# A two-layer DeltaNet, S5 and MLA backbone with experts: other order of the first loads, of the merged projections, and of the loads behind the first experts

## Chip, cores, metric

The kernel runs on one core of a Trainium2 chip. The metric is the device time of one execution, in microseconds (us), as the median of several runs. A profile of one execution shows what each engine did: TensorE (PE), VectorE (DVE), ScalarE (ACT), GpSimd (POOL), SyncE (SP, which here only issues DMAs), and the 16 DMA engines behind them.

## What is computed

Two layers over 256 latent and 256 context tokens of width 1024, four tiles of 128 tokens in all. Every sub-layer is modulated by shift, scale and gate vectors that come from a small condition vector through a large weight (`ada_w`, 2 x 1024 x 6144).

```python
for i in range(2):
    sh1, sc1, g1, sh2, sc2, g2 = adaln(c, ada_w[i], ada_b[i])     # silu(c) @ ada_w + ada_b, cut in six
    h = rmsnorm(x, norm1_g[i]) * (1 + sc1) + sh1
    if i == 0:      # gated DeltaNet heads beside S5 channel groups, both directions, one output projection
        o = mixer_ab(h_ctx, h_lat, w_in, conv_w, ..., A_re, A_im, log_dt, B, C, D, glu_w, glu_b, w_out)
    else:           # latent attention
        o = mixer_mla(h_ctx, h_lat, w_in, q_norm_g, w_q_up, kv_norm_g, w_kv_up, w_out, cos, sin)
    x = x + g1 * o
    x = x + g2 * grouped_moe(modulate(x), router_w, router_bias, w_gate, w_up, w_down)  # 16 experts, top 2
return rmsnorm(x, final_norm_g)
```

## The kernel before, in words

The program runs through stages, whose bounds in the profiled execution are about these.

- **Start, 0 to 45 us.** `norm0()` normalises and transposes the four token tiles. `ada_gen(0, 0)` loads the first third of layer 0's `ada_w` in 16 chunks of 512 KB (`ch<-in_ada_w`, issued by SP in `load_chunk`) and multiplies each by the condition, which stands in `stat`. `stat` is a copy (L239) of `sg`, which ACT computes from `condT` (L238). `s5_base()` is a long chain of small DVE instructions on the S5 constants `sA` and `sBC`, and ends with `bcr` and `bci`. Behind that chain, in DVE's order, stands `adaev` (L272): the finished modulation plus its bias `adab`, from which PE makes the columns `mcols`. With these DVE and ACT modulate the tokens and the first projection can start on PE.
- **Merged projections, 45 to 345 us.** Five generators (U and S5 tables, S5 matmuls, DeltaNet projections and convolutions, gates, and `loads`, which is the other `ada_gen` parts) are taken one step at a time in the order that the digits of `ORDER` give (`merge`). That order is the order in which each engine gets its instructions. `adab` is filled by two DMAs (L258) ahead of each part, added at the part's end (L272) or, for the part that is cut in two, at its cut (L269).
- **Inverses, 305 to 383 us.** DVE runs a recursion of 31 steps on small triangles (L880 multiplies, L882 reduces; the row lengths grow from step to step up to 961), then two stream transposes (L886, L887), whose result DVE, ACT and POOL copy into `DT` (L1022). `gth` are four gate tiles of the S5 readout (PE, then ACT L972, DVE L973 and L974, POOL stores them, L975). `PI` are starting matrices for the solve (L1040). SP loads the matrices `A` (L1047), `dec` and `qe` in the memory that earlier tiles held, so that its first such load waits for the last DVE read of `gth`.
- **Solve, scan, output projection, routing, 345 to 600 us.**
- **Experts of layer 0, 600 to 875 us.** Weight chunks `ch<-in_wg`, `in_wu`, `in_wd` of 1 MB stream in through SP. A unit writes its result to DRAM by an indirect store (`yd<-y,rt`, L1769). At the end `combine()` loads four tiles `y` of 1 MB back from there, through POOL's queue (L1699), adds their halves on POOL (L1700) and scales and adds them on DVE. The last pair of experts is not stored: its two down weights are multiplied (`down`), and `put_back` spreads the product over the tokens. `open_rg2()` loads the MLA's input weight (`in_mla_w_in`, 4 chunks of 704 KB).
- **MLA, 875 to 1000 us, and experts of layer 1, to 1288.8 us.**

DMAs that are issued by SP and ACT take turns on eight semaphores (in the rows `DMAHW0` to `DMAHW7`), and those of POOL on eight others (`DMASW`): the next DMA on a semaphore is issued only when the one before it has landed. Lines of the changed kernel are one or two higher than those of the kernel before.

Of the kernel before, what the change touches and what calls it, by code (L numbers as in the profile page):

```python
# [10 lines left out]
F32 = mybir.dt.float32  # L11
# [27 lines left out]
ARB = 3  # L39
EA = 0  # L40
HG = (2, 5)
ORDER = "31031442142040140344004440342042144241140004011240243042313341044002441404410432024401434324021044244444244334104124204010344040301240440214420003444442204322414144304030404014104423444410441104234444144032440214301440024230"


def const_arrays():
# [115 lines left out]
def build(tc, I, O):  # L161
    with ExitStack() as es:
        _build(es, tc, I, O)


def _build(es, tc, I, O):
    nc = tc.nc
    V, S, G, T = nc.vector, nc.scalar, nc.gpsimd, nc.tensor

    per = es.enter_context(tc.tile_pool(name="per", bufs=1))  # L170
# [5 lines left out]
    def nm(s):  # L176
        cnt[0] += 1
        return f"{s}_{cnt[0]}"
# [3 lines left out]
    def ps(tag=None):  # L182
        if tag is None:
            tag = banks[0] % banks[1]
            banks[0] += 1
        return psum.tile([128, 512], F32, tag=f"ps{tag}", name=nm("ps"))
# [4 lines left out]
    def chunk(dt=F32):  # L191
        pool = slots[0][slots[1] % len(slots[0])]
        slots[1] += 1
        return pool.tile([128, width[0]], dt, tag="ch", name=nm("ch"))

    def load_chunk(src, shape, eng=nc.sync):
        n = 1
        for s in shape[1:]:
            n *= s
        v = chunk()[:, :n]  # L200
        three = v.rearrange("p (a b) -> p a b", a=shape[1]) if len(shape) == 3 else v
        eng.dma_start(v if len(src.shape) == 2 else three, src)
        return three

    def tp(out, in_, n=128):
        T.transpose(out, in_, ident[:n, :n])

    def mm(out, l, r, start, stop):
        return T.matmul(out, l, r, start=start, stop=stop)  # L209
# [4 lines left out]
    def bcast_rows(src_row, n, parts=128):  # L214
        return bass.AP(tensor=src_row.tensor, offset=src_row.offset, ap=[[0, parts], [1, n]])


    cm = per.tile([128, 7 * 128], F32, name="cm")
    nc.scalar.dma_start(cm, I["c_mats"])
    ident, triF, triB, triS, ones, nmF, nmB = (cm[:, i * 128:(i + 1) * 128] for i in range(7))  # L220
    sm = per.tile([128, 432], F32, name="sm")
    nc.scalar.dma_start(sm, I["c_small"][:, 0:432])
    neghalf = sm[:, SM_NH:SM_NH + 1]
    condT = per.tile([128, 16], F32, name="condT")
    nc.scalar.dma_start(condT, I["condT"])


    def rsqrt(pool, out, ss, n, scale, eps):
        t = pool.tile([128, n], F32, tag=f"rs{n}", name=nm("rs"))
# [10 lines left out]
    adab = per.tile([128, 512], F32, name="adab")  # L240
# [2 lines left out]
    rope = per.tile([128, 2, 2, 32], F32, name="rope")  # L243
    mg = per.tile([128, 5], F32, name="mg")
    n1g = per.tile([128, 2, 8], F32, name="n1g")
    nc.scalar.dma_start(n1g.rearrange("p a b -> p (a b)"), I["norm1_g"])
    mcols = per.tile([128, 2, 2, 2, 8], F32, name="mcols")
    cols1 = per.tile([128, 2, 8], F32, name="cols1")

# [4 lines left out]
    def ada_gen(l, th, ks=range(KD), eng=lambda k: nc.sync):  # L254

        if ks[0] == 0:
            for c in range(2):
                nc.scalar.dma_start(adab[c:128:32, :], I["ada_b"][l, th])  # L258
        p = ps(3)
        for k in ks:  # L260
            for c0 in range(0, 2048, width[0]):
                w = load_chunk(I["ada_w"][l, k * 128:(k + 1) * 128, th * 2048 + c0:th * 2048 + c0 + width[0]],
                               [128, width[0]], eng(k))
                for j in range(width[0] // 512):
                    jj = c0 // 512 + j
                    mm(p[32 * jj:32 * jj + 32, :], stat[:, k, :], w[:, j * 512:(j + 1) * 512], k == ks[0], k == ks[-1])
                yield
        if ks[-1] < KD - 1:
            V.tensor_tensor(adab, p, adab, op=OP.add)  # L269
            return  # L270
        ev = per.tile([128, 512], F32, tag="adaev", name=nm("adaev"))
        V.tensor_tensor(ev, p, adab, op=OP.add)  # L272
        if th == 0:
            p = ps()
            for b in range(4):
                tp(p[:, b * 128:(b + 1) * 128], ev[:, b * 128:(b + 1) * 128])
            pv = p.rearrange("p (b j r) -> p j b r", b=4, j=4)
            for c in range(2):
                V.tensor_copy(mcols[:, l, c, 1].rearrange("p (j b) -> p j b", j=2), pv[:, 0:2, :, c])
                V.scalar_tensor_tensor(mcols[:, l, c, 0].rearrange("p (j b) -> p j b", j=2), pv[:, 2:4, :, c], 1.0,  # L280
                                       n1g[:, l].rearrange("p (j b) -> p j b", j=2), op0=OP.add, op1=OP.mult)
            return
        for c in range(2):
            (nc.scalar if (l, th) == (1, 2) else G).dma_start(modd[l, c, th * 2048:(th + 1) * 2048].rearrange("(j n) -> j n", n=512),
ev[c:128:32, :])
# [42 lines left out]
    def merge(order, *gens):  # L328

        for c in order:  # L330
            next(gens[int(c)], None)
        rr(*gens)
# [5 lines left out]
    def seq(*gens):  # L338
        for g in gens:
            yield from g  # L340
# [50 lines left out]
    qT, kT = (gp.tile([128, 4, 512], F32, tag=n, name=n) for n in ("qT", "kT"))  # L391
    rnq = gp.tile([128, NT, 4], F32, name="rnq")
    convw = gp.tile([128, 12, 5], F32, name="convw")
    nc.scalar.dma_start(convw.rearrange("p a b -> p (a b)"), I["conv_w"])
    gbr = gp.tile([128, 16], F32, name="gbr")
    nc.scalar.dma_start(gbr, bcast_rows(I["gate_b"], 16))
    dng = gp.tile([128, 1], F32, name="dng")
    nc.scalar.dma_start(dng, I["dn_g"].rearrange("a p -> p a"))

    def g32(n):  # L400
        return gp.tile([128, NT, 8], F32, name=n)
# [13 lines left out]
    sp1 = s5st.enter_context(tc.tile_pool(name="sp1", bufs=1, side="right"))  # L415
    sp2 = s5st.enter_context(tc.tile_pool(name="sp2", bufs=2, side="right"))
    sA = sp1.tile([128, 96], F32, name="sA")
    nc.scalar.dma_start(sA, I["s5_A"])
    sBC = sp1.tile([128, 1024], F32, name="sBC")
    nc.scalar.dma_start(sBC, I["s5_BC"])  # L420
    sDl = sp1.tile([128, 8], F32, name="sDl")
    nc.scalar.dma_start(sDl, I["s5_Dl"])
    are, aim = sA[:, 0:32], sA[:, 32:64]
    bcr = sp1.tile([128, 544], F32, name="bcr")
    bci = sp1.tile([128, 544], F32, name="bci")
# [205 lines left out]
    with tc.tile_pool(name="xi1", bufs=1) as xi1, tc.tile_pool(name="ar", bufs=ARB) as arp:  # L631
# [23 lines left out]
        for k in range(KD):  # L655
            for c in range(2):
                a, b = mcols[:, 0, c, 0, k:k + 1], mcols[:, 0, c, 1, k:k + 1]
# [332 lines left out]
    with tc.issue_after(mark.ins):  # L990
        G.memset(X, 0.0)
        rr(with_loads(proj_u()), s5_tables(0))
    yT = pj.tile([128, 4, 512], F32, tag="uy", name="yT")
    merge(ORDER,
          seq(s5_run(0), s5_run(1), s5_run(2), s5_run(3), glu()),
# [20 lines left out]
    for j in range(2):  # L1016
        for d in range(2):
            for b in range(4):
                g0, u0, s_ = 64 * d + 32 * (b // 2), 16 * (b % 2), slice(32 * b, 32 * b + 32)
                src = (Lt if j ^ d else LX)[g0:g0 + 32].rearrange("p k u -> p u k")[:, u0:u0 + 16, :]  # L1020
# [591 lines left out]
    wi, rg2s = [], []  # L1612

    def open_rg2():

        rg2 = es.enter_context(tc.tile_pool(name="rg2", bufs=RG2))
        old, i = slots
        slots[0], slots[1] = [rg2] * RG2, 0
        for j in range(4):
            wi.append(load_chunk(I["mla_w_in"][j], [128, 2, 704]))  # L1620
        slots[0], slots[1] = old, i
        return rg2


    def experts0(m):
        with ExitStack() as st:
# [194 lines left out]
            p = [p for _, _, p in down(cur)]  # L1821
            put_back(p, m.tokf[:, cs], tokm[:, cs], m.gate[:, cs])
            w3s.close()
            rg2s.append(open_rg2())
            last = [rg2s[0].tile([128, 4, 512], F32R, tag="ch", name=f"ch{i}") for i in "hl"]

            def two():
# [208 lines left out]
    with tc.tile_pool(name="l1h", bufs=1) as lh, tc.tile_pool(name="l1i", bufs=2) as li:  # L2036
# [4 lines left out]
        for t in range(NT):  # L2041
            if t + 1 < NT:
                norm_T(1, li, x, hT1, (t + 1,))
            p = ps()
# [22 lines left out]
            p = ps()  # L2067
# [9 lines left out]
            if t >= 2:  # L2077
                p = ps()
# [157 lines left out]
```

## Time and profile before

| | |
|---|---|
| median of 3 runs | 1289.83 us (1289.03 to 1290.67) |
| profiled execution: time | 1290.54 us |
| profiled execution: span of its trace | 1288.8 us |
| PE busy | 1122.1 us (87%) |
| DVE busy | 707.3 us (55%) |
| ACT busy | 437.2 us (34%) |
| POOL busy | 322.1 us (25%) |
| moved by DMA | 340.30 MB, 264 GB/s over the span |
| DMA queue q1 (SP and ACT loads of large rows) / q10 (small rows) / q0 (POOL) | 306.25 / 17.41 / 15.50 MB |

The time of an execution is 1.7 us more than the span, from the first to the last instruction that the trace holds. PE is the busiest engine, but its share is an average over stages: it is near its limit in the merged projections and the experts, and waits at the start, in the inverses and at the end of the first experts.

### The profile page before, as it was taken

How to read it: one execution, taken by the hardware profiler on the slowest of the kernel's cores; microseconds unless marked ns; L12 is line 12 of the kernel's file. 1: busy time of each engine (PE TensorE's matmuls, PEld its weight loads, DVE VectorE, ACT ScalarE, POOL GpSimd, SP SyncE). 2: the span in 40 equal slices, each digit the busy share in tenths (PEclk: the TensorE clock that was granted, in tenths of full speed). 3: DMA queues.
4: the chain of work that ended last, by engine and by line, in shares of the span. 5: the costliest groups of instructions: out<-in, count | busy, mean ns of one | idle time of the engine just before them, and what ended most of it. 6: DMA issues, size and time to landing. Idle time of an engine off the chain costs nothing. (4 is left out here: it accounts for less than half of the span.)

```text
span 1288.8 us, 17198 instructions
## 1 busy us (share of the span) xinstructions
PE 1122.1 (87%) x6208; PEld 706.1 (55%) x6208; DVE 707.3 (55%) x1452; ACT 437.2 (34%) x763; POOL 322.1 (25%) x263
## 2 busy tenths in 40 slices
PE   4698999999759998769999999867999949999985
PEld 1365566565229987626567577325777735444321
DVE  3979796847694564742347478245576260223122
ACT  3323535352123242213446467205455111111101
POOL 0355453321236330312133233133321010000000
PEclk9799999999878998879999999978999959999998
DMA  9565576887738154658999999753134758999992
GB/s 329 196 196 179 198 225 204 251 289 227 223 129 279 59 187 148 253 201 361 399 380 418 396 419 388 268 221 121 59 124 148 292 220 356 417 419 421 420 421 123
DMA packets 101784, 340.30 MB, mean 264 GB/s; under 512 B 26806, under 2 KB 44598, under 8 KB 75328
## 3 DMA queue, kind: packets, MB, share of 16 engines
q1 hardware_dynamic: 75792, 306.25, 62.9%
q10 hardware_dynamic: 20128, 17.41, 4.3%
q0 software_dynamic: 5776, 15.50, 3.1%
q8 instruction: 51, 0.84, 0.3%
q14 instruction: 37, 0.30, 0.1%
HBM read 318.40 MB, written 25.72 MB: 267 GB/s over the span
## 5 line engine op out<-in xcount | busy, mean ns | idle before, releaser
L1684 DVE TENSOR_TENSOR lo<-ch,hi 128x1024 fp32r<-128x1024 f32 x80 | 112.1, 1443 | 57.2 <-ACT hi L1682 57.1
L209 PE MATMUL ps<-hi,sp 128*128 128x512 f32 x432 | 112.4, 399 | 1.3 <-ACT y L1767 1.3
L209 PE MATMUL ps<-ch,stat 128*32 128x512 f32 x384 | 89.3, 652 | 24.3 <-DVE stat L239 14.0
L209 PE MATMUL ps<-ch,xT 128*64 128x512 f32 (+1 forms) x488 | 108.7, 596 | 1.3 <-DMA ch<-in_wg 1.3
L209 PE MATMUL ps<-ch,wh 128*64 128x512 f32 x384 | 100.9, 631 | 6.7 <-SPq L1592 6.7
L1682 ACT ACTIVATE hi<-ch 128x1024 fp32r<-128x1024 f32 x96 | 94.3, 1056 | 35.5 <-DMA ch<-in_wg 27.3
L209 PEld LDWEIGHTS ps<-hi,sp 128*128 128x128 f32 x432 | 79.4, 188 | 27.1 <-issue 5.7
L209 PE MATMUL ps<-hH,wh 128*128 128x512 f32 x160 | 66.2, 415 | 5.9 <-ACT hH L664 5.1
L209 PE MATMUL ps<-hH,wl 128*128 128x512 f32 x160 | 65.2, 408 | 1.6 <-DVE wl L611 1.6
L209 PE MATMUL ps<-hL,wh 128*128 128x512 f32 x160 | 65.7, 410 | 0.4 <-POOL hL L665 0.2
L209 PE MATMUL ps<-lo,sp 128*128 128x512 f32 x216 | 63.7, 403 | 2.5 <-DVE lo L1684 1.5
L209 PEld LDWEIGHTS ps<-ch,xT 128*64 128x64 f32 (+1 forms) x488 | 33.3, 129 | 59.3 <-issue 55.2
L209 PEld LDWEIGHTS ps<-ch,wh 128*64 128x64 f32 x384 | 28.9, 144 | 65.7 <-issue 62.1
L1684 POOL TENSOR_TENSOR lo<-ch,hi 128x1024 fp32r<-128x1024 f32 x16 | 42.4, 2647 | 87.2 <-ACT hi L1682 62.9
L231 POOL TENSOR_TENSOR frs<-rs,sm 128x1 f32<-128x1 f32 x2 | 1.1, 548 | 241.2 <-DVE rs L230 241.2
L209 PE MATMUL ps<-ch,aT 128*64 128x512 f32 (+1 forms) x232 | 55.9, 613 | 3.9 <-DMA ch<-in_wd 3.2
L209 PEld LDWEIGHTS ps<-lo,sp 128*128 128x128 f32 x216 | 39.1, 188 | 16.7 <-issue 3.2
L611 POOL TENSOR_TENSOR wl<-raw,wh 128x1024 fp32r<-128x1024 f32 x16 | 39.7, 2479 | 27.7 <-ACT wh L610 27.6
L1919 DVE SCALAR_TENSOR_TENSOR y<-ps,rt,bcm 128x512 f32<-128x512 f32 x14 | 10.5, 752 | 65.2 <-PE ps L209 65.2
L1151 POOL TENSOR_TENSOR ch<-ch,ch 128x512 fp32r<-128x512 f32 (+1 forms) x28 | 31.8, 1165 | 53.7 <-PE ps L209 29.9
L748 DVE SCALAR_TENSOR_TENSOR ac<-ps,convw,ac 128x510 f32<-128x510 f32 (+1 forms) x48 | 35.6, 741 | 13.3 <-ACT ac L744 12.9
L209 PEld LDWEIGHTS ps<-ch,stat 128*32 128x32 f32 x384 | 12.9, 113 | 54.3 <-DMA ch<-in_ada_w 24.8
(542 smaller groups left out, 2368.6 us busy)
## 6 DMA issues: line engine op xcount, KB each, us to landing
ch<-in_wg SPq DMA_DIRECT2D x63, 1024.0 KB, 13.7
ch<-in_wu SPq DMA_DIRECT2D x62, 1024.0 KB, 10.2
ch<-in_wd SPq DMA_DIRECT2D x61, 1024.0 KB, 12.2
ch<-in_ada_w SPq DMA_DIRECT2D x88, 512.0 KB, 4.8
raw<-in_w_in SPq DMA_DIRECT2D x16, 512.0 KB, 3.5
bcm<-modd ACTq DMA_DIRECT2D x12, 512.0 KB
x<-in_xs SPq DMA_DIRECT2D x8, 512.0 KB, 8.2
yd<-x SPq DMA_DIRECT2D x8, 512.0 KB, 4.9
```

What stands on the lines that cost most here:

```text
L209: return T.matmul(out, l, r, start=start, stop=stop)
L231: G.tensor_tensor(out, t, bc(neghalf, [128, n]), op=OP.pow)
L611: eng.tensor_tensor(wl, w, wh.bitcast(F32), op=OP.subtract)
L748: V.scalar_tensor_tensor(ac[:, :, lo:hi], pv[:, :, lo + o:hi + o], convw[:, blk, j:j + 1], ac[:, :, lo:hi], op0=OP.mult, op1=OP.add)
L1151: eng.tensor_tensor(lo, src, hi.bitcast(F32), op=OP.subtract)
L1682: S.activation(hi[:, s], w[:, s], AF.Copy)
L1684: e.tensor_tensor(lo[:, s], w[:, s], hi[:, s].bitcast(F32), op=OP.subtract)
L1919: V.scalar_tensor_tensor(y, p, j.gate, g2[:, nh * 512:(nh + 1) * 512], op0=OP.mult, op1=OP.mult)
```

## The change

There are three parts.

1. The condition `condT` is issued as the first DMA of ACT's queue, ahead of `cm` and `sm`. Seven small constants (`n1g`, `convw`, `gbr`, `dng`, `sA`, `sBC`, `sDl`) and the twelve `adab` loads are issued by POOL in place of ACT.
2. `ORDER` is another string with the same number of each digit (50, 30, 30, 24 and 90 of 0 to 4).
3. The four `in_mla_w_in` loads are issued after the last load of `in_wd`, through `issue_after`.

```diff
-ORDER = "31031442142040140344004440342042144241140004011240243042313341...
+ORDER = "41040414313243010242003024140101404241444403141443434244404024...
...
+    issued = [None]
+
     def load_chunk(src, shape, eng=nc.sync):
...
-        eng.dma_start(v if len(src.shape) == 2 else three, src)
+        issued[0] = eng.dma_start(v if len(src.shape) == 2 else three, src)
...
+    condT = per.tile([128, 16], F32, name="condT")
+    nc.scalar.dma_start(condT, I["condT"])
     cm = per.tile([128, 7 * 128], F32, name="cm")
     nc.scalar.dma_start(cm, I["c_mats"])
...
-    condT = per.tile([128, 16], F32, name="condT")
-    nc.scalar.dma_start(condT, I["condT"])
-
...
-    nc.scalar.dma_start(n1g.rearrange("p a b -> p (a b)"), I["norm1_g"])
+    G.dma_start(n1g.rearrange("p a b -> p (a b)"), I["norm1_g"])
...
             for c in range(2):
-                nc.scalar.dma_start(adab[c:128:32, :], I["ada_b"][l, th])
+                G.dma_start(adab[c:128:32, :], I["ada_b"][l, th])
...
-    nc.scalar.dma_start(sA, I["s5_A"])
+    G.dma_start(sA, I["s5_A"])
...
-    nc.scalar.dma_start(sBC, I["s5_BC"])
+    G.dma_start(sBC, I["s5_BC"])
...
-            rg2s.append(open_rg2())
+            with tc.issue_after(issued[0].ins):
+                rg2s.append(open_rg2())
```

**ACT at the program's start.** The rows are ACT's instructions in their order, before; what stands in brackets is what an instruction waits for.

```order
L219 DMA cm<-in_c_mats 128x896
L222 DMA sm<-in_c_small 128x432
L225 DMA condT<-in_condT 128x16
L246 DMA n1g<-in_norm_g 128x16
L394 DMA convw<-in_conv_w 128x60 [waits DMAHW1_49]
L396 DMA gbr<-in_gate_b 128x16 [waits DMAHW3_49]
L398 DMA dng<-in_dn_g 128x1 [waits DMAHW5_49]
L418 DMA sA<-in_s_A 128x96 [waits DMAHW7_49]
L420 DMA sBC<-in_s_BC 128x1024 [waits DMAHW1_49]
L238 ACT_TABLE_LOAD
L238 ACTIVATE sg<-condT 128x16
```

The same place of the changed kernel:

```order
L221 DMA condT<-in_condT 128x16
L223 DMA cm<-in_c_mats 128x896
L226 DMA sm<-in_c_small 128x432
L239 ACT_TABLE_LOAD
L239 ACTIVATE sg<-condT 128x16 [waits DMAHW0_49]
L291 ACTIVATE junk_157,ss_155<-x_144 128x1024 [waits DMAHW1_49]
L1982 DMA rope<-in_c_rope 128x128
```

Five DMAs that wait for earlier DMAs stood ahead of `sg`; now none does. The seven constants stand at the head of POOL's order, without a wait, and a pair of `adab` loads stands behind them.

**DVE around the `adab` addition.** The rows are DVE's, before, in the late steps of the recursion (`x_144` holds the triangles).

```order
L880 TENSOR_TENSOR x_144<-x_144 128x484
L882 TENSOR_REDUCE x_144<-x_144 128x22
L269 TENSOR_TENSOR adab<-ps_2953,adab 128x512
L880 TENSOR_TENSOR x_144<-x_144 128x529
L882 TENSOR_REDUCE x_144<-x_144 128x23
```

In the changed kernel:

```order
L881 TENSOR_TENSOR x_144<-x_144 128x676
L270 TENSOR_TENSOR adab<-ps_2904,adab 128x512
L883 TENSOR_REDUCE x_144<-x_144 128x26
L881 TENSOR_TENSOR x_144<-x_144 128x729
L883 TENSOR_REDUCE x_144<-x_144 128x27
```

The addition stood after step 22; now three whole steps and half of a fourth (23 to 26) stand ahead of it.

**DVE at the end of the recursion.** Before, from the last multiplication on:

```order
L880 TENSOR_TENSOR x_144<-x_144 128x961
L974 TENSOR_TENSOR gth_3287<-yT,gth_3287 128x512
L882 TENSOR_REDUCE x_144<-x_144 128x31
L1040 COPY PI_3359<-cm 128x512
L1040 COPY PI_3363<-cm 128x512
L973 TENSOR_SCALAR gth_3297<-gth_3297 128x512
L886 STREAM_TRANSPOSE x_144<-x_144 128x1024
L887 STREAM_TRANSPOSE x_144<-x_144 128x1024
L974 TENSOR_TENSOR gth_3297<-yT,gth_3297 128x512
L1022 COPY DT<-x_144 32x16x32 x4
```

In the changed kernel:

```order
L883 TENSOR_REDUCE x_144<-x_144 128x31
L887 STREAM_TRANSPOSE x_144<-x_144 128x1024
L888 STREAM_TRANSPOSE x_144<-x_144 128x1024
L974 TENSOR_SCALAR gth_3287<-gth_3287 128x512
L1023 COPY DT<-x_144 32x16x32 x4
L1041 COPY PI_3359<-cm 128x512
L975 TENSOR_TENSOR gth_3287<-yT,gth_3287 128x512
L1041 COPY PI_3363<-cm 128x512
L974 TENSOR_SCALAR gth_3297<-gth_3297 128x512
L975 TENSOR_TENSOR gth_3297<-yT,gth_3297 128x512
```

The two `PI` copies and half a `gth` pair no longer stand ahead of the transposes; the last two `gth` pairs now stand behind the `DT` copies. On ACT the `gth_3297` activation (L973) has moved behind ACT's eight `DT` copies in the same way.

**SP at the end of the first experts.** Before (the `ISA` rows put an expert's number in an address):

```order
L202 DMA ch_6699<-in_wu 128x2048
L202 DMA ch_6803<-in_mla_w_in 128x1408
L202 DMA ch_6805<-in_mla_w_in 128x1408
L202 DMA ch_6807<-in_mla_w_in 128x1408
L202 DMA ch_6809<-in_mla_w_in 128x1408
L202 ISA
L202 DMA ch_6740<-in_wd 128x2048
```

In the changed kernel:

```order
L204 DMA ch_6740<-in_wd 128x2048
L204 ISA
L204 DMA ch_6742<-in_wd 128x2048
L204 ISA
L204 DMA ch_6753<-in_wd 128x2048
L204 ISA
L204 DMA ch_6755<-in_wd 128x2048
L204 DMA ch_6803<-in_mla_w_in 128x1408
```

The four down weights are now issued ahead of the four mixer weights. The first mixer load waited for PE and DVE (its memory is that of the experts' last split weights); the first down weight waits for one of these DVE instructions, not for PE.

## Rows read from the trace of the kernel before

**Rows 1.** Windows: bounds, length, busy PE PEld DVE ACT POOL (x), PEclk, DMA share, GB/s

```profile
100.00:200.00 100.00, 93.29 (x748) 62.10 (x748) 84.13 (x161) 43.90 (x95) 52.17 (x41) 1.00 0.60 194
...
345.00:400.00 55.00, 34.38 (x159) 20.96 (x158) 41.47 (x45) 17.42 (x27) 26.69 (x21) 0.78 0.59 204
...
830.00:875.00 45.00, 25.45 (x62) 7.68 (x58) 19.28 (x21) 0.66 (x2) 12.97 (x8) 0.78 0.56 229
```

**Rows 2.** Timeline of ACT and its queue at the start: start, length, engine, line

```profile
1.65 0.45 ACTq L225 DMA_DIRECT2D condT<-in_condT  x1
...
13.50 0.21 ACT L238 ACTIVATE sg<-condT 128x16 f32<-128x16 f32 x1
```

**Rows 3.** Timeline of PE at the start (in brackets: idle before, releaser)

```profile
13.98 1.94 PE L209 MATMUL ps<-ch,stat 128*32 128x512 f32 x8 [13.98 <-DVE stat L239]
...
39.59 1.05 PE L209 MATMUL ps<-ch,stat 128*32 128x512 f32 x4 [0.21 <-DMA ch<-in_ada_w]
```

**Rows 4.** Timeline of DVE at the start, first and last of the chain

```profile
22.03 0.17 DVE L347 TENSOR_SCALAR exdt<-sA 128x32 f32<-128x32 f32 x1
...
43.28 0.68 DVE L272 TENSOR_TENSOR adaev<-ps,adab 128x512 f32<-128x512 f32 x1
```

**Rows 5.** Windows as in rows 1: the start, and a stretch of weight loading

```profile
4.00:40.00 36.00, 19.46 (x94) 6.14 (x96) 19.35 (x106) 12.85 (x21) 2.21 (x4) 1.00 0.96 354
...
830.00:840.00 10.00, 4.15 (x16) 1.27 (x12) 0.69 (x1) 0.60 (x1) 2.91 (x4) 0.91 1.01 416
```

**Rows 6.** Timeline of POOL, its first weight split

```profile
45.69 2.39 POOL L611 TENSOR_TENSOR wl<-ch,wh 128x1024 fp32r<-128x1024 f32 x1 [3.49 <-ACT wh L610]
```

**Rows 7.** Timeline of DVE in the recursion's late steps

```profile
353.09 0.69 DVE L269 TENSOR_TENSOR adab<-ps,adab 128x512 f32<-128x512 f32 x1 [7.87 <-DMA ch<-in_glu_w]
...
360.98 0.86 DVE L882 TENSOR_REDUCE x<-x 128x26 f32<-128x676 f32 x1
...
373.74 0.42 DVE L973 TENSOR_SCALAR gth<-gth 128x512 f32<-128x512 f32 x1
...
375.81 0.68 DVE L974 TENSOR_TENSOR gth<-yT,gth 128x512 f32<-128x512 f32 x1
...
377.48 2.55 DVE L1040 COPY PI<-cm 128x512 f32<-128x512 f32 x2
...
380.28 1.89 DVE L886 STREAM_TRANSPOSE x<-x 128x1024 f32<-128x1024 f32 x1
```

**Rows 8.** Timelines of ACT, SP and DVE behind the transposes

```profile
374.08 0.69 ACT L972 ACTIVATE gth<-ps,glub 128x512 f32<-128x512 f32 x1 [3.02 <-DMA c5d<-gth]
...
382.26 8.54 ACT L1022 COPY DT<-x 32x512 f32<-32x512 f32 x8 [6.44 <-DVE x L886]
...
383.97 0.38 SPq L1047 DMA_DIRECT2D A<-atd  x1
...
391.49 0.69 DVE L1082 TENSOR_TENSOR dec<-ps,dec 128x512 f32<-128x512 f32 x1 [2.19 <-DMA dec<-dcd]
```

**Rows 9.** Timelines of SP and POOL at the end of the first experts

```profile
825.38 2.04 SPq L202 DMA_DIRECT2D ch<-in_mla_w_in  x4
827.62 4.26 SPq L202 DMA_DIRECT2D ch<-in_wd  x4
...
826.35 0.97 POOL L1769 DMA_INDIRECT yd<-y,rt  x1 [6.28 <-ACT y L1767]
835.48 2.91 POOL L1699 DMA_DIRECT2D ch<-yd  x4 [8.16 <-issue]
847.72 2.34 POOL L1700 TENSOR_TENSOR ch<-ch 128x1024 f32<-128x1024 f32 x1 [9.32 <-DMA ch<-yd]
```

**Rows 10.** POOL's twelve indirect stores: from issue to landing

```profile
DMA to landing us min/median/max: 4.2/9.2/13.3
```

**Rows 11.** What PE waited for (60 to 345 us), and who waited for `adab` loads

```profile
PE ps L209 <- DMA ch<-in_ada_w: 6.0, 7, 2.9
...
  ACT vt L750: 9.8, 1
```

More of the change, by code (lines that the diff above doesn't have):

```diff
@@ L41 @@
 HG = (2, 5)
-ORDER = "31031442142040140344004440342042144241140004011240243042313341044002441404410432024401434324021044244444244334104124204010344040301240440214420003444442204322414144304030404014104423444410441104234444144032440214301440024230"
+ORDER = "41040414313243010242003024140101404241444403141444434244404024011202020010013333444144244340402442214333040144420001444414402120400440240432041400242344403004041344444414231420440044444414114343442210204014240240143442403320"
 def const_arrays():
@@ L393, in _build @@
     convw = gp.tile([128, 12, 5], F32, name="convw")
-    nc.scalar.dma_start(convw.rearrange("p a b -> p (a b)"), I["conv_w"])
+    G.dma_start(convw.rearrange("p a b -> p (a b)"), I["conv_w"])
     gbr = gp.tile([128, 16], F32, name="gbr")
-    nc.scalar.dma_start(gbr, bcast_rows(I["gate_b"], 16))
+    G.dma_start(gbr, bcast_rows(I["gate_b"], 16))
     dng = gp.tile([128, 1], F32, name="dng")
-    nc.scalar.dma_start(dng, I["dn_g"].rearrange("a p -> p a"))
+    G.dma_start(dng, I["dn_g"].rearrange("a p -> p a"))
     def g32(n):
@@ L417, in _build @@
     sA = sp1.tile([128, 96], F32, name="sA")
-    nc.scalar.dma_start(sA, I["s5_A"])
+    G.dma_start(sA, I["s5_A"])
     sBC = sp1.tile([128, 1024], F32, name="sBC")
-    nc.scalar.dma_start(sBC, I["s5_BC"])
+    G.dma_start(sBC, I["s5_BC"])
     sDl = sp1.tile([128, 8], F32, name="sDl")
-    nc.scalar.dma_start(sDl, I["s5_Dl"])
+    G.dma_start(sDl, I["s5_Dl"])
     are, aim = sA[:, 0:32], sA[:, 32:64]
```

## Prediction

> **What bounds the kernel now.** I read the busy time by windows first, then the timelines at the three places that the change touches, then the table of waits between them. In the windows [rows 1] the reader is to see that the stages differ: in the merged projections PE is busy 93.29 of 100 us, so what comes earlier there stays earlier; from 345 to 400 us it is busy 34.38 of 55 and from 830 to 875 us 25.45 of 45, so there something else ends last. The first 45 us are a race between loads and a DVE chain. ACT reaches `sg` only at 13.50 although `condT` was issued at 1.65 [rows 2], and PE begins at 13.98 [rows 3]. That idle time is not the loss, though. PE then catches up with the loads: its last chunk at 39.59 waits for a DMA again [rows 3]. The end of the stage is `adaev` at 43.28 [rows 4], 2.64 us after that chunk's matmuls end (39.59 + 1.05), because DVE first has to finish the S5 constants, a dense chain that starts at 22.03 and is 21.25 us long up to `adaev`.
>
> **Part 1, the start.** Moving instructions off ACT's queue lets `sg` go as soon as `condT` lands. What this is worth is set by the later of two ends.
> DVE's chain: `sA` is the fifth POOL DMA, and POOL takes 2.91 / 4 = 0.73 us to issue one [rows 9], so it leaves at about 0.7 + 5 x 0.73 = 4.4. No row shows how soon such a load lands; the nearest are POOL's indirect stores, 4.2 to 13.3 us [rows 10]. So the chain starts between 8.6 and 17.7 and gets to `adaev` between 29.9 and 39.0, in either case ahead of 40.64. The 2.64 us go.
> Loads: from 4 to 40 us 36 us at 354 GB/s = 12.7 MB were moved, with the DMA engines busy 0.96 of the time [rows 5]. If only the idle 4% can be won, the last chunk comes 1.4 us earlier; if the rate rises to the 416 GB/s of the later stretch [rows 5], 12.7 MB take 30.6 us, 5.4 less. SP will have fewer waits on shared semaphores, but the same small rows travel; I take 3.0. Sum of part 1: 2.64 + 3.0 = about 5.5 us, with 0 (the loads no faster and the chain late) and 8 as ends.
> What it adds: a pair of `adab` loads on POOL, waiting for DVE to read the old `adab`, now stands ahead of POOL's first weight split. The split itself waited for ACT until 45.69 [rows 6], 2.41 us after `adaev` began; `adaev`'s 0.68 and two issues of 0.73 make 2.14, so ACT's wait covers it. If ACT too came earlier by 1 us, the cost would be 0.7. I take nothing for it.
> At this point the Trainium skill speaks against the change. "DMA: Bandwidth & Descriptors" (Rules for kernel authors) says that spreading DMAs over several issuing engines buys no bandwidth, since all share the same 16 DMA engines, and saves only issue time. By that rule the load term would be near the 1.4 us of idle share and part 1 would be worth 4.0; the 0.96 is a row that leans to it, and it is the second rival's ground below.
>
> **Part 2, the new ORDER.** PE's work is the same and nearly in the same places, so I cost the inverses' end, where DVE is behind. Before, DVE stood 7.87 us at the `adab` addition, until 353.09, for the last `ada_w` matmuls [rows 7]. Now the steps that ran from 353.78 (353.09 + 0.69) to 360.98 [rows 7], 7.2 us, stand ahead of it, so the wait shrinks to 0.7. From 377.48 to 380.28 two `PI` copies and a `gth` half stood ahead of the transposes, 2.8 us, and the pair of `gth_3287` (0.42 + 0.68 at most, 0.9 with their overlap) moves behind too [rows 7]. The transposes so start 7.2 + 2.8 + 0.9 = 10.9 us earlier, at 369.4 on the old time scale.
> Most of this goes back. SP's first `A` load left at 383.97 [rows 8], when DVE had read the last `gth`. ACT copies `DT` for 8.54 us, from 2.0 us after the first transpose starts (382.26 against 380.28) [rows 7, 8]; `gth_3297` now stands behind these copies. So: 369.4 + 2.0 + 8.5 = 379.9 for ACT's copies, 0.7 for the `gth` activation [rows 8], 1.1 for its two DVE instructions, and `A` leaves at 381.7 instead of 383.97. What the solve waits for behind it, down to `dec` at 391.49, which waits for a load issued after `A` [rows 8], follows by the same 2.3 us. Lower end: the new sequence can cost PE waits elsewhere. PE lost 6.0 us to `ada_w` chunks between 60 and 345 us [rows 11], and a redrawn order moves these either way; I give it half of them, 3. Upper end: 10.9 if ACT's `gth` does not hold `A`, which the order excludes; 5.3 with a gain in the projections. I take 2.5, from -1 to 5.5.
>
> **Part 3, the mixer's loads.** Before, SP stood at the first `in_mla_w_in` until 825.38, and the four down weights left from 827.62 on [rows 9]. The store issued at 826.35 met this burst: POOL came to its four `y` loads 8.16 us after issuing it, at 835.48 [rows 9], while the shortest of the twelve stores landed in 4.2 [rows 10]. The first sum of `y` began at 847.72 [rows 9], and PE's spreading and DVE's additions to 875 stand behind it. Now the first down weight leaves once DVE's split is done, before PE's end at 825.4, the others follow as PE frees their buffers, and the mixer's 2.8 MB (4 x 704 KB) come last. So the store has the DMA engines nearly alone for its first 2 us; I estimate 4.7 us instead of 8.2, so `y` leaves and the chain behind it runs 3.5 us earlier. Ends: 8.16 - 4.2 = 4.0; and 0, or a loss of 1, if the down weights now share with the store as the mixer's did. The mixer's weights come later, but have some 45 us until the norm ends; this cover holds.
>
> **Sum.** 5.5 + 2.5 + 3.5 = 11.5 us off the profiled 1290.54 gives 1279.0; its own median was 0.7 lower, so I forecast 1278.5 us.
>
> **Rivals.**
> - *Only part of it* (0.22). The start stays bound by its loads (4.0 or less), and either the merge's gain or the store's comes to nothing. For it: the share of 0.96 and the 8.5 us that part 2 hands back. Against it: three independent terms. 1289.8 - 3 to 8 us: 1282 to 1287, in the middle 1284.5.
> - *More* (0.10): loads at 416 GB/s (8), merge 5.5, store 4.0, so 17.5 off: 1272; with a clock on PE that doesn't fall around 345 us (PEclk is 0.78 there [rows 1]) down to 1268.
> - *No change* (0.08): the freed time reappears as waiting in the projections, within 0.2%, 2.6 us, about what a measurement of this kernel can tell.
> - *Slower* (0.12): POOL's queue. An `adab` load waits for DVE to read the old bias; before, it held ACT for 9.8 us once [rows 11], and ACT had nothing urgent. On POOL it holds weight splits, which take 2.39 us [rows 6] and feed PE. Five more pairs are issued; two stand directly ahead of a split. If each holds its split by 9.8 us less the 2.4 that ACT's wait covers, PE loses 14.8 us against 11.5 won: 1293. It decides once such waits sum to over 11.5 us. Against it: the waits are at the end of an `ada_gen` part, and most other splits are spread well apart from these.
> The Trainium skill has a second mechanism for this rival: "SBUF — State Buffer" (SBUF: two separate sides) says that while DVE runs certain copies GpSimd cannot write descriptors, so that DMAs from its queue stand still. No run here shows it yet; it would lengthen the same holds.
>
> **How the numbers follow.** The forecast's case, a gain of 8 to 16 us, 1274 to 1282, has 0.48. With 0.10 above and 0.22 below, faster by over 0.2% has 0.80, the same 0.08, slower 0.12. A range of 1269 to 1287 leaves out the slower case, most of the unchanged one and little of the largest gains, about 2 in 10.
>
> **What would show it.** Start: `sg` before 8 us, the DVE chain done before the last chunk, `adaev` at 37 to 39 us and released by PE. Inverses: the wait at the `adab` addition under 2 us, transposes directly behind the last step, and `A` released by `gth_3297`, some 12 us behind the transposes. End of experts: down weights from 822 on, the store landed within 5 us, the first sum at about 844 less the earlier gains. Wrong would be: `adaev` still released by DVE's own order, PE waiting for `wl` behind an `adab` issue on POOL, or the store still at 8 us beside the down weights.

## The result, and the profile after the change

| | before | after |
|---|---|---|
| median (lowest to highest, 7 runs each) | 1289.83 us (1281.38 to 1295.66) | 1281.9 us (1277.56 to 1286.09) |
| profiled execution, time / span | 1290.54 / 1288.8 us | 1283.03 / 1281.2 us |

The ratio is 0.9947, with a 95% interval from 0.9923 to 0.9971: 6.8 us of 1289.83, faster by more than 0.2%. The forecast was 1278.5 us.

The two traces, read at the same instructions, give this account (the last column is what each stretch adds to the gain):

| instruction | before | after | gained so far | in this stretch |
|---|---|---|---|---|
| `adaev`, DVE | 43.28 | 43.09 | 0.2 | |
| first projection, PE | 50.28 | 49.69 | 0.6 | 0.6 |
| first stream transpose, DVE | 380.28 | 366.91 | 13.4 | 12.8 |
| first load of `A`, SP | 383.97 | 380.51 | 3.5 | -9.9 |
| routing starts, DVE | 539.35 | 535.45 | 3.9 | 0.4 |
| last store of the first experts, POOL | 826.35 | 819.98 | 6.4 | 2.5 |
| `y` loads, POOL | 835.48 | 823.74 | 11.7 | 5.3 |
| first matmul of the MLA's norm, PE | 877.89 | 867.22 | 10.7 | -1.0 |
| routing of layer 1, PE | 1029.56 | 1020.23 | 9.3 | -1.4 |
| end of the span | 1288.8 | 1281.2 | 7.6 | -1.7 |

**The start.** ACT's timeline, against [rows 2], then PE's [rows 3] and DVE's [rows 4]:

```profile
5.25 0.21 ACT L239 ACTIVATE sg<-condT 128x16 f32<-128x16 f32 x1 [1.82 <-DMA condT<-in_condT]
15.31 1.06 ACT L291 ACTIVATE junk<-x 128x1024 bf16<-128x1024 f32 x1 [1.80 <-DMA x<-in_xs]
16.36 4.25 ACT L641 ACTIVATE x<-x,rs 128x1024 f32<-128x1024 f32 x4
...
16.73 1.92 PE L211 MATMUL ps<-ch,stat 128*32 128x512 f32 x4 [16.73 <-DVE rs L231]
40.21 1.05 PE L211 MATMUL ps<-ch,stat 128*32 128x512 f32 x4 [0.23 <-DMA ch<-in_ada_w]
...
16.56 0.15 DVE L231 TENSOR_SCALAR rs<-ss 128x1 f32<-128x1 f32 x1 [1.48 <-ACT junk L291]
16.63 0.17 DVE L348 TENSOR_SCALAR exdt<-sA 128x32 f32<-128x32 f32 x1
20.66 0.69 DVE L646 COPY x<-ps 128x512 f32<-128x512 f32 x1 [2.75 <-ACT x L641]
22.88 0.69 DVE L646 COPY x<-ps 128x512 f32<-128x512 f32 x1 [1.21 <-PE ps L208]
23.76 0.69 DVE L646 COPY x<-ps 128x512 f32<-128x512 f32 x1
26.90 0.69 DVE L646 COPY x<-ps 128x512 f32<-128x512 f32 x1 [1.34 <-PE ps L208]
43.09 0.68 DVE L273 TENSOR_TENSOR adaev<-ps,adab 128x512 f32<-128x512 f32 x1
```

`sg` goes 8.25 us earlier, and DVE's chain starts 5.4 us earlier, yet `adaev` is where it was. Copies of transposed tokens (L646) stand in DVE's order between the chain's instructions. Before the change the first of them was done ahead of the chain, and the other three stood inside it without a wait of their own:

```profile
21.15 0.69 DVE L645 COPY x<-ps 128x512 f32<-128x512 f32 x1
24.45 0.68 DVE L645 COPY x<-ps 128x512 f32<-128x512 f32 x1
26.46 0.69 DVE L645 COPY x<-ps 128x512 f32<-128x512 f32 x1
28.47 0.69 DVE L645 COPY x<-ps 128x512 f32<-128x512 f32 x1
```

Now the chain has come to them before the tokens are ready. It waits 2.75 + 1.21 + 1.34 = 5.3 us for normalisations (L641) that all stand behind ACT's sum of squares of the fourth token tile (15.31). From its first instruction to `adaev` it takes 26.46 us instead of 21.25, and the difference is about these waits. The chain's own start, too, is set by that tile: the `rs` ahead of it (16.56) waits for the same sum, while `sA`, issued at 3.63, had landed 8.5 us later. PE's first `ada_w` matmul is not held by DVE, whose `stat` copy was done at 5.7; the `rs` that its row names only ended last. Its chunk, issued at 5.24, took 11.4 us to land. The matmul begins 2.75 us later than before, and the last chunk comes at 40.21 instead of 39.59. The window against [rows 5]:

```profile
4.00:40.00 36.00, 20.01 (x92) 6.48 (x92) 19.79 (x106) 11.77 (x20) 4.78 (x12) 0.95 0.95 347
```

The loads moved at 347 GB/s against 354, with the DMA engines busy 0.95 against 0.96 of the time.

**The inverses.** DVE's and ACT's timelines, SP's first load, and PE's first matmul with `A`, against [rows 7, 8]:

```profile
350.35 0.69 DVE L270 TENSOR_TENSOR adab<-ps,adab 128x512 f32<-128x512 f32 x1 [2.20 <-PE ps L211]
366.91 1.90 DVE L887 STREAM_TRANSPOSE x<-x 128x1024 f32<-128x1024 f32 x1
...
368.88 5.32 ACT L1023 COPY DT<-x 32x512 f32<-32x512 f32 x5 [3.31 <-DMA Kn<-knd]
374.22 3.25 ACT L1023 COPY DT<-x 32x512 f32<-32x512 f32 x3
377.49 0.69 ACT L973 ACTIVATE gth<-ps,glub 128x512 f32<-128x512 f32 x1
...
379.75 0.69 DVE L975 TENSOR_TENSOR gth<-yT,gth 128x512 f32<-128x512 f32 x1
380.51 0.38 SPq L1048 DMA_DIRECT2D A<-atd  x1
383.51 2.05 PE L211 MATMUL ps<-DT,A 128*128 128x128 f32 x8 [16.72 <-DMA A<-atd]
```

The reader sees the handing back in four rows: the transposes at 366.91, ACT's `DT` copies to 377.47, the `gth` that waited behind them, and `A` 13.6 us behind the transposes, where before it was 3.7.

**The end of the first experts.** SP and POOL, against [rows 9]:

```profile
815.81 9.70 SPq L204 DMA_DIRECT2D ch<-in_wd  x4
...
819.98 0.97 POOL L1770 DMA_INDIRECT yd<-y,rt  x1 [6.28 <-ACT y L1768]
823.74 2.91 POOL L1700 DMA_DIRECT2D ch<-yd  x4 [2.78 <-issue]
836.03 2.33 POOL L1701 TENSOR_TENSOR ch<-ch 128x1024 f32<-128x1024 f32 x1 [9.38 <-DMA ch<-yd]
841.83 2.35 POOL L1701 TENSOR_TENSOR ch<-ch 128x1024 f32<-128x1024 f32 x1 [3.47 <-DMA ch<-yd]
```

POOL's wait for the store fell from 8.16 to 2.78 us. The first sum still waits 9.38 us for its loads, and the next ones now wait too.

### The profile page after: what moved, and what is told of

Read it like the earlier page. It is cut to its first block, busy times and chain, and to the rows that moved or that the text cites. A ratio compares the mean times of both kernels' runs of the same rounds, so it can differ in the third digit from the quotient of the medians.

```text
span 1281.2 us, 17228 instructions
## 1 busy us (share of the span) xinstructions
PE 1116.6 (87%) x6208; PEld 705.5 (55%) x6208; DVE 705.8 (55%) x1452; ACT 439.2 (34%) x764; POOL 332.7 (26%) x282
## 5 line engine op out<-in xcount | busy, mean ns | idle before, releaser
L211 PE MATMUL ps<-ch,wh 128*64 128x512 f32 x384 | 95.6, 604 | 0.7 <-ACT wh L1664 0.7
L211 PEld LDWEIGHTS ps<-ch,stat 128*32 128x32 f32 x384 | 13.6, 116 | 64.2 <-issue 32.5
L1152 POOL TENSOR_TENSOR ch<-ch,ch 128x512 fp32r<-128x512 f32 (+1 forms) x28 | 31.5, 1155 | 53.8 <-PE ps L211 29.9
```

The lines of the kernel that those rows point to most:

```text
L1152: eng.tensor_tensor(lo, src, hi.bitcast(F32), op=OP.subtract)
```

## The experiments

Each was timed beside the kernel before on the same chip; the change itself is in the last row. The kernel before had medians of 1289.82 us beside the first four rows, 1289.70 beside the next four and 1288.42 beside the four after them, so medians from different groups compare less well than ratios. The ratio is not the quotient of two medians, and the two can differ by 2 or 3 us. "Noted" columns are from the profiled execution: first projection on PE, first transpose on DVE, first `DT,A` matmul on PE, routing on DVE, and the `y` loads on POOL.

| kernel | median us (runs) | ratio to before, 95% | projection | transpose | `DT,A` | routing | `y` loads |
|---|---|---|---|---|---|---|---|
| only part 1 | 1296.34 (12) | 1.0044 [1.0022, 1.0065] | 49.47 | 377.55 | 395.40 | 548.01 | 848.05 |
| only part 2 | 1296.8 (12) | 1.0045 [1.0022, 1.0069] | 52.26 | 384.65 | 397.57 | 551.71 | 845.59 |
| only part 3 | 1287.33 (12) | 0.9958 [0.9932, 0.9983] | 50.64 | 384.85 | 391.24 | 543.73 | 831.08 |
| parts 2 and 3 | 1292.12 (12) | 1.0020 [0.9991, 1.0049] | 52.42 | 381.14 | 393.94 | 547.65 | 835.98 |
| all, `dec` x3 | 1279.74 (9) | 0.9928 [0.9902, 0.9954] | 49.01 | 371.30 | 375.52 | 534.63 | 822.97 |
| before, `dec` x3 | 1286.27 (12) | 0.9986 [0.9962, 1.0010] | 50.52 | 380.37 | 387.08 | 539.43 | 833.72 |
| part 1, `dec` x3 | 1288.49 (12) | 0.9997 [0.9973, 1.0020] | 49.49 | 380.10 | 385.30 | 543.91 | 837.83 |
| all, mixer behind `y` | 1281.75 (12) | 0.9946 [0.9924, 0.9969] | 50.15 | 365.26 | 382.23 | 535.77 | 827.57 |
| all, copies on ACT | 1284.67 (12) | 0.9969 [0.9950, 0.9989] | 47.45 | 366.40 | 383.30 | 536.26 | 830.99 |
| all, `dec` x3, copies on ACT | 1278.03 (6) | 0.9913 [0.9884, 0.9941] | 48.30 | 372.41 | 376.62 | 535.02 | 823.34 |
| parts 2 and 3, `dec` x3 | 1286.5 (12) | 0.9976 [0.9950, 1.0002] | 50.20 | 377.72 | 382.97 | 543.38 | 838.42 |
| all, `adab` on ACT | 1286.54 (12) | 0.9990 [0.9965, 1.0015] | 47.20 | 376.93 | 389.80 | 540.47 | 828.85 |
| all (the change) | 1281.9 (7) | 0.9947 [0.9923, 0.9971] | 49.69 | 366.91 | 383.51 | 535.45 | 823.74 |

**The parts apart.** Four kernels with one or two of the three parts of the change:

```diff
 only part 1: the kernel before, and
+    condT ahead of cm and sm; G.dma_start for seven constants and adab
 only part 2: the kernel before, and
+ORDER = "41040414313243010242003024140101404241444403141443434244404024...
 only part 3: the kernel before, and
+            with tc.issue_after(issued[0].ins):
+                rg2s.append(open_rg2())
 parts 2 and 3: the changed kernel, with part 1 taken back
```

Part 1 alone: 

> The kernel before with part 1 alone (condition first, small constants on POOL's queue). Theory A, from the two traces: the DVE chain starts earlier but then stands behind the four token copies, adaev comes at about 43 as before, so ratio 0.999 to 1.001, under 1.5 us. Theory B, as predicted: 5.5 us, ratio 0.996, with adaev at 37 to 39.

Part 2 alone: 

> The kernel before with the new ORDER alone. Theory A: 2 to 3.5 us faster, ratio 0.9975; the transposes start 10 us or more earlier, the first A load only 2 to 3.5 us earlier. Theory B (the trace's gain up to 345 us was chance or came from part 1): ratio 1.000.

Part 3 alone: 

> The kernel before with the mixer's loads behind the down weights alone. Theory A: POOL's wait for the last store shrinks from 8.2 to about 3 us and the time falls by 4 to 5.5 us, ratio 0.996. Theory B (the y loads and not the store set the end, what is won is given back behind the mixer's later weights): under 1.5 us.

Parts 2 and 3: 

> The changed kernel without part 1 (old start, new ORDER, mixer's loads behind the down weights). Theory A: as fast as the full change within 1.5 us, ratio to the kernel before 0.994 to 0.996. Theory B, part 1 pays in the full change: slower than it by 3 us or more, ratio 0.997 or above.

Only part 3 pays by itself: 5.4 us by the ratio (1289.82 x 0.0042), with 2.2 to 8.8 us by its interval, while the medians differ by 2.5. Its place shows the same mechanism as in the changed kernel, a wait of 2.77 us between the last store and the `y` loads. Part 1 alone and part 2 alone make the kernel 5.7 and 5.8 us slower, and parts 2 and 3 together are not told from before. Added up, the three parts give 6 us in the wrong direction; together they give 6.8 us. The idea that the parts add fell; parts 1 and 2 without part 3 were not run. The theories missed the time of part 1 alone and of part 2 alone, since none had a loss; in the place the first theory of part 1 held, with `adaev` at 42.87. For part 3 the first theory held, for parts 2 and 3 the second. The profiled execution of part 1 alone was the slowest of its twelve (1303.92), so its trace shows the places better than the sizes. Part 1 alone loses behind the transposes, where ACT and SP of that kernel show

```profile
389.97 0.69 ACT L973 ACTIVATE gth<-ps,glub 128x512 f32<-128x512 f32 x1
392.19 0.38 SPq L1048 DMA_DIRECT2D A<-atd  x1
395.40 2.04 PE L211 MATMUL ps<-DT,A 128*128 128x128 f32 x8 [8.78 <-DMA A<-atd]
```

The last `gth` stands behind ACT's `DT` copies there without any new `ORDER`, and `A` goes 14.6 us after the transposes. Part 2 alone keeps the two `PI` copies ahead of its transposes (at 384.65), so `ORDER` alone does not bring the sequence that the prediction costed.

**The wait of `A` for `gth`.** The first `A` lies in memory that the readout's tiles held. `dec`, which shares its pool, had four buffers; with three, `A`'s address moves out of there:

```diff
-        dec = eA.tile([128, 4, 128], F32, tag="dec", name=nm("dec"))
+        dec = eA.tile([128, 4, 128], F32, tag="dec", bufs=3, name=nm("dec"))
```

In the changed kernel: 

> The changed kernel with three buffers for dec in place of four, so that the memory of the first A load no longer reaches into that of yT, which the last gth addition reads. Theory A (A's wait for the last gth addition sets the end of the inverses): the first A load leaves before 345 us instead of 380.5, the first solve matmul starts at 377 to 379 instead of 383.5, when the DT copies are done, and the time falls by 4 to 6 us, ratio to the kernel before 0.990. Theory B (the solve is bound by the DT copies and the PI matrices anyway): under 1.5 us below the change, ratio 0.994.

In the kernel before: 

> The kernel before with three buffers for dec. There A left 3.7 us behind the transposes and ACT's DT copies ended at 390.8, after A's landing at 386.9. Theory A: the copies take over the wait, 0 to 2 us faster, ratio 0.999. Theory B (the loads, wherever they stand, cost the same): 4 us or more faster, ratio 0.997 or less.

With part 1 alone: 

> The kernel before with part 1 alone and three buffers for dec. Theory A (part 1 alone loses because the old ORDER then puts the last gth addition 14.6 us behind the transposes): 5 to 7 us faster than part 1 alone, ratio to the kernel before 0.999 in place of 1.0044. Theory B (it loses in the projections): ratio 1.003 or more.

The load leaves at 339.87, 348.12 and 354.07 in the three kernels. In the changed kernel PE's and DVE's timelines become

```profile
375.52 2.05 PE L211 MATMUL ps<-DT,A 128*128 128x128 f32 x8 [5.07 <-ACT DT L1023]
379.80 2.05 PE L211 MATMUL ps<-DT,A 128*128 128x128 f32 x8 [2.23 <-DVE DT L1023]
386.29 2.04 PE L211 MATMUL ps<-PI,DT 128*128 128x128 f32 x8 [4.44 <-DVE PI L1072]
...
383.76 1.73 DVE L975 TENSOR_TENSOR gth<-yT,gth 128x512 f32<-128x512 f32 x1
385.41 0.73 DVE L1072 COPY_PREDICATED PI<-lvl,ps 128x512 f32<-128x512 int32 x1
```

The first `DT,A` matmul is 8.0 us earlier than in the changed kernel, although the transposes come 4.4 us later here (371.30 against 366.91). The matmul with `PI` is only 2.3 us earlier (388.54 there): the wait moves to the `DT` copies and then to DVE, where the same `gth` now stands ahead of `PI`. Routing is 0.8 us earlier, the medians differ by 2.2 us, between the two theories, and the intervals overlap. Before the change the copies end as late as `A`, so the edit gives nothing at this place (387.08 against 386.90). With part 1 alone it wins 10.1 us there (395.40 to 385.30) and 4.1 us at routing, and the ratio goes from 1.0044 to 0.9997. So most of what part 1 loses alone goes when `A` is freed, and the wait of `A` is the likely place; the edit moves other instructions too, such as the transposes from 377.55 to 380.10.

**Parts 2 and 3 with `A` freed.** The same line of `dec` in the kernel with parts 2 and 3:

> Parts 2 and 3 without part 1, and dec in three buffers. Theory A (ORDER without part 1 loses only at A's wait for the last gth): as dec3, with the start of the kernel before, so 1280.5, ratio 0.993. Theory B (it loses ahead of the inverses, since the same string gives the engines another order when the DMAs of part 1 are on other queues): the transposes stay near 381 instead of 367, routing comes near 545 instead of 535, and the time is about 1289, ratio 0.999.

The second theory held in the place: the transposes come at 377.72, 10.8 us behind the change, and routing at 543.38, 7.9 us behind. In the time the ratio of 0.9976 rules out the first theory's 0.993. But `A` counts here as well: against parts 2 and 3 without the edit, the first `DT,A` matmul comes 11.0 us earlier (393.94 to 382.97), routing 4.3 us earlier, and the ratio falls from 1.0020 to 0.9976, though the intervals overlap. Without part 1 the new `ORDER` loses ahead of the inverses, and, as far as these two runs show, at `A` too. The profiled execution was the slowest of its twelve (1295.64, median 1286.50).

**Which piece of part 1 the `ORDER` needs.** In the changed kernel, only the `adab` loads go back to ACT:

```diff
-                G.dma_start(adab[c:128:32, :], I["ada_b"][l, th])
+                nc.scalar.dma_start(adab[c:128:32, :], I["ada_b"][l, th])
```

> The changed kernel with only the twelve adab loads back on ACT's queue; condT stays first and the seven constants stay on POOL. Theory A (what ORDER needs of part 1 is the adab loads, which recur through the merged projections, on POOL): the transposes come at 375 to 381 as without part 1, and the time is 1290 to 1292, ratio 1.000 to 1.002. Theory B (it needs the start alone): transposes at 367, adab's addition with a wait of 2 us, ratio 0.995.

The first theory held in the place and about in the size, if with a time somewhat below what it gave: transposes at 376.93 in place of 366.91, and no gain that can be told from zero, although this kernel has the earliest first projection of all (47.20). Its DVE has the two `PI` copies ahead of the transposes again, and PE waits twice as long for `ada_w` chunks between 45 and 345 us. DVE's timeline and PE's waits of this kernel, and behind the dots PE's waits of the changed one (total, times, longest):

```profile
374.33 2.69 DVE L1041 COPY PI<-cm 128x512 f32<-128x512 f32 x2
376.93 1.89 DVE L887 STREAM_TRANSPOSE x<-x 128x1024 f32<-128x1024 f32 x1
...
PE ps L211 <- DMA ch<-in_ada_w: 12.4, 12, 2.0
...
PE ps L211 <- DMA ch<-in_ada_w: 6.1, 8, 2.8
```

SP shows a likely cause: here it stands up to 12.6 us at one staging store (L863, in the rows a wait for the tile `x`), in the changed kernel 2.4 at most. The three other kernels with the new `ORDER` and without the `adab` loads on POOL show the same pair: up to 10.8 to 12.5 us at that store, and 10.0 to 10.7 us of PE's waits for `ada_w` chunks. No run changes the store alone. The program is built with `schedule_with_timeline_sim=True` (L2232 of the kernel before): a scheduler draws each engine's order from its own model of the times, so an `ORDER` string can mean another order on the engines as soon as a DMA changes its queue, as DVE's order does here.

**The chain at the start.** In the changed kernel the four copies of tokens that DVE makes go to ACT; the orders of PE, POOL and SP stay the same:

```diff
-                    (V.tensor_copy if h else S.copy)(hT[:, 4 * h:4 * h + 4, t], h4(p))
+                    S.copy(hT[:, 4 * h:4 * h + 4, t], h4(p))
```

> The changed kernel with the four DVE copies of transposed tokens at the start (L646) put on ACT beside ACT's own four; the orders of PE, POOL and SP are the same as in the changed kernel. Theory A (part 1 gained so little because these copies, and the waits ahead of them, stand inside DVE's S5 chain): the chain loses 2.8 us of copies and 5.3 us of waits, adaev is released by PE right behind the last ada_w chunk at about 41.4 us instead of 43.09, the first projection starts near 48.0 instead of 49.69, and the time falls by 1.7 us to about 1280.2 (ratio 0.993). Theory B (the chain is held elsewhere, or the start is covered behind): adaev stays at 43, or comes earlier without any change of the time (0.9947).

With `dec` in three buffers too:

> The kernel before this one with dec in three buffers as well, so that the load of A needs no memory of gth. If the two gains are independent (theory A): 1281.9 - 2.2 - 1.7 = 1278.0, ratio 0.991, below both kernels. If what is won at the start is lost in the merged projections or at the transposes (theory B): 1279.7 as with dec alone, ratio 0.993.

DVE and PE of the first of these:

```profile
37.57 0.68 DVE L490 TENSOR_TENSOR bci<-bci,tmpb 128x512 f32<-128x512 f32 x1
40.90 0.69 DVE L273 TENSOR_TENSOR adaev<-ps,adab 128x512 f32<-128x512 f32 x1 [2.65 <-PE ps L211]
47.45 1.22 PE L211 MATMUL ps<-hH,wh 128*128 128x512 f32 x2 [5.15 <-ACT hH L665]
```

The chain ends at 38.25, and PE releases `adaev`, as the first theory had it; the first projection is 2.24 us earlier, of which some 0.4 us are the loads', whose last chunk came at 39.80 in this execution. The time did not follow: 0.9969 is no better than 0.9947, and the intervals overlap. Of the 2.24 us 0.8 are left at the third `adaev`, 0.5 at the transposes and 0.2 at the first `DT,A` matmul, so the merged projections take the start's gain back. With `dec` in three buffers the median is the lowest of all, 1278.03 us of only 6 runs, ratio 0.9913; whether the copies add to `dec` (1279.74) is open, since both lie within the other's interval. Both versions have lower medians than the change, and clearly lower than the kernel before.

**The mixer's loads behind the `y` loads.** POOL issues both, one behind the other:

```diff
-            with tc.issue_after(issued[0].ins):
-                rg2s.append(open_rg2())
+            with tc.issue_after(ylast.ins):
+                rg2s.append(open_rg2(G))
```

> The changed kernel with the mixer's four loads issued by POOL behind its four y loads, in place of SP behind the down weights. Theory A (the y loads, which share the DMA engines with the mixer's 2.8 MB, set the end of the first experts): the last y sum starts 5 to 7 us earlier, the norm of the MLA too, ratio to the kernel before 0.990. Theory B (only the store's landing counts): no change against 0.9947, or a loss if the mixer's weights come too late for the MLA.

```profile
827.57 2.94 POOL L1700 DMA_DIRECT2D ch<-yd  x4 [2.78 <-issue]
830.51 2.13 POOL L204 DMA_DIRECT2D ch<-in_mla_w_in  x4
838.71 2.33 POOL L1701 TENSOR_TENSOR ch<-ch 128x1024 f32<-128x1024 f32 x1 [6.08 <-DMA ch<-yd]
841.27 8.84 POOL L1701 TENSOR_TENSOR ch<-ch 128x1024 f32<-128x1024 f32 x3 [0.23 <-DMA ch<-yd]
```

Here the sum's wait falls from 9.38 to 6.08 us and the other sums follow without a gap, 3 us won at this place; the time is the change's, 0.9946 to 0.9947. In this execution the store came 3.8 us later for another reason (last section). Up to the first matmul of the MLA's norm the 3 us are kept: it begins at 867.92, 0.7 us behind the change. Why the medians show nothing of them stays open.

## Why the prediction was right, and where it was not

The time was right: 1281.9 us against 1278.5, between 1269 and 1287, and faster. The sum of 11.5 us that made it came out as 6.8 to 7.9, and one of its three terms failed. That the time still lies well inside the range is partly luck: in the two traces part 3 gave 1.8 us more than predicted, and 2.2 us came from the landing of a load that the change does not touch (last section).

**Part 1 (5.5 us predicted, 0.6 in the trace).** Two steps failed. "So the chain starts between 8.6 and 17.7 and gets to `adaev` between 29.9 and 39.0": it started at 16.63, inside these bounds, but not for their reason: `sA` had landed at about 12.1, and the fourth token tile held the chain. And its length did not stay 21.25 us. Of the four token copies three stood inside it before as well, but there the tokens were ready; started earlier, it waits 5.3 us for them. The experiment with the copies on ACT shows that these copies and their waits were all that kept `adaev` behind PE. The prediction's own sign of being wrong, `adaev` still released by DVE's own order, is what the trace shows. "I take 3.0" for the loads: the last chunk came 0.6 us later instead of 3.0 earlier. On this the rule of "DMA: Bandwidth & Descriptors" (Rules for kernel authors) of the Trainium skill, that more issuing engines buy no bandwidth, was the better guide, and the trace agrees: 347 GB/s after, 354 before. The 1.4 us that the idle share would have allowed did not come either. Nor does "what comes earlier there stays earlier" hold in the merged projections: with the copies on ACT they gave back 1.7 of the 2.24 us up to the transposes. That the term adds to the others failed as well: alone, part 1 costs 5.7 us, most of which goes when `A` is freed.

**Part 2 (2.5 us predicted).** The mechanism was as written: the addition's wait shrank from 7.87 to 2.20 us, the transposes came 13.4 us earlier (10.9 predicted; the addition itself was also 2.7 us earlier, 350.35 against 353.09), ACT's `DT` copies held the last `gth`, and 9.9 us were handed back. `A` moved by 3.5 us and routing by 3.9, of which 0.6 are the start's, so 3.3 against 2.5. But the term was put down to `ORDER`, and `ORDER` alone is 5.8 us slower: what was priced is the engine order that `ORDER` and part 1's queues give together. The share of 1 and 2 together is 6.8 - 5.4 = 1.4 us, with an uncertainty of several us.

**Part 3 (3.5 us predicted, 5.3 in the trace, 5.4 alone).** Right in mechanism, and too small; 5.3 lies above the term's own upper end of 4.0. The store's landing was estimated at 4.7 us from the shortest of twelve [rows 10], and POOL waited for it 2.78. Part of this is a mixed measure: the 8.16 us of [rows 9] count from the end of the store's issue, which takes 0.97 us, and the landings of [rows 10] from its start. That the down weights left early, at 815.81, is as predicted.

**The rivals.** *Only part of it* is nearest to what happened, and for its reason at the start: the loads did not come sooner. Its other condition, that the merge's gain or the store's comes to nothing, is not what the trace shows. *Slower* by POOL's queue is refuted. The nine `adab` loads between 45 and 345 us landed 2.4 to 5.6 us after their issue, POOL waited ahead of one of them for 4.9 us, and PE's waits in that stretch hold none for POOL. Whether the block on GpSimd's DMAs that "SBUF — State Buffer" (SBUF: two separate sides) of the Trainium skill describes played a part is not shown: a hold of up to some 3 us (5.6 - 2.4) could stand in these landings. The loss that this kernel could have had was elsewhere, in an `ORDER` without its queues: 5.8 us, not among the rivals.

**What was not predicted.** 2.5 us came at the first experts' weights and 4.1 us went back behind the `y` loads, of which 1.0 ahead of the MLA's norm and 1.7 behind the routing of layer 1. The last section has the first of these; the others were not followed further.

## What to carry to other kernels

A long chain that starts earlier does not keep its length: look for what stands inside it, and ask whether that will be ready by then. An order that a scheduler draws is a joint product of the order string and of every queue; price the parts together or time them apart, and don't put a gain down to one of them. When a wait is removed at a place where several things are late within a few us of each other (`A`, the `DT` copies, `PI`), expect the difference to the next one, not the wait.

## What the runs showed of the hardware that was not expected

The landing of one load differs between the profiled executions by as much as a part of this change. The first 1 MB chunk of `in_wg` behind layer 0's routing is issued by SP, and ACT's first split waits for it. In the changed kernel, the one with the mixer behind `y` and the one with the copies on ACT, SP's issues and ACT's splits read

```profile
553.54 14.30 SPq L204 DMA_DIRECT2D ch<-in_wg  x2
559.46 2.01 ACT L1683 ACTIVATE hi<-ch 128x1024 fp32r<-128x1024 f32 x2 [24.04 <-DMA ch<-in_wg]
...
553.91 17.78 SPq L204 DMA_DIRECT2D ch<-in_wg  x2
562.23 2.00 ACT L1683 ACTIVATE hi<-ch 128x1024 fp32r<-128x1024 f32 x2 [26.49 <-DMA ch<-in_wg]
...
554.40 20.66 SPq L204 DMA_DIRECT2D ch<-in_wg  x2
564.61 2.00 ACT L1683 ACTIVATE hi<-ch 128x1024 fp32r<-128x1024 f32 x2 [28.38 <-DMA ch<-in_wg]
```

From issue to split these are 5.9, 8.3 and 10.2 us, and the 14 profiled kernels lie between 5.9 and 10.2 (before: 8.1). PE, POOL and SP have the same order in the first and the third. Of the 7.6 us between the two spans, 8.1 - 5.9 = 2.2 are of this kind, and so is most of the 2.5 us in the table at the last store. Three of the 14 lie over 10 us: the copies on ACT (10.2), part 1 alone (10.1) and parts 2 and 3 with `dec` x3 (10.1). These are also the three whose profiled execution was the slowest of its twelve, 4.3 to 9.1 us over the median, which suggests that the landing goes with the execution and not with the kernel. Why it varies was not tried.

TensorE's granted clock differs between executions too. Part 3 alone has PE's order of the kernel before. Its windows, and behind the dots those of before:

```profile
125.00:130.00 5.00, 1.85 (x12) 0.56 (x12) 5.00 (x11) 0.86 (x1) 3.88 (x3) 0.94 0.56 121
130.00:135.00 5.00, 5.00 (x19) 1.84 (x19) 4.05 (x11) 4.14 (x5) 0.65 (x1) 0.50 0.77 262
135.00:140.00 5.00, 5.00 (x22) 4.08 (x21) 5.00 (x13) 1.26 (x3) 2.48 (x3) 0.53 0.63 241
...
125.00:130.00 5.00, 4.17 (x29) 2.34 (x30) 5.00 (x12) 1.36 (x2) 1.29 (x2) 1.00 0.88 290
130.00:135.00 5.00, 5.00 (x24) 3.20 (x24) 4.04 (x7) 3.36 (x4) 2.38 (x1) 1.00 0.34 129
```

PE stood 3.15 us at a load of `Tq` there, and behind it the granted clock was 0.50 and 0.53, which is the lower level of 1.2 GHz, for nearly 10 us; before, the wait at the same matmul was 2.31 us and the clock stayed at 1.00, 2.4 GHz. That the wait brought the lower clock is read from this pair, not tried. The stretch cost 4.4 us in place: the execution was 4.0 us behind at the matmul with `Tq` (129.85 against 125.83) and 8.4 us at one of the projections behind it (139.72 against 131.32). Of these 8.4 us 4.0 are made up by routing (543.73 against 539.35), so how much of the lag there is the clock's is not shown.

So a few us between two traces far from an edit need not be its effect; the ratios carry the comparisons of time above, and the traces only the places.
